# All rows of the array for the spread of the decay sums and for the decay gate's products

## The chip, the cores and the metric

The kernel runs on one core of a Trainium2 chip, in one launch. The metric is the device time in microseconds; lower is better. Before the change the median of three runs is 1002.88 us (1002.50 to 1004.13).

## What is computed

Two transformer blocks in a row on 256 tokens of width 1024, in float32. The change lies in the second block's mixer, which adds two recurrent mixers of one projection `n @ w_in`: a state-space one (SSD, 16 heads in 2 groups) and a gated linear attention (GLA, 4 heads of 128 keys).

```python
proj = n @ w_in                                   # x, z, q, k, v, r, a1 (16 columns), dt (16 columns), ...
# SSD: dt = softplus(dt_raw + dt_bias); a = -dt * exp(A_log); a_cs = cumsum of a over the chunk
#   L[l, s] = exp(a_cs[l] - a_cs[s]) for l >= s, per head
#   y = (C B^T * L) @ (x * dt) + C @ state * exp(a_cs)
# GLA:
log_alpha = jax.nn.log_sigmoid((a1 @ w_a2 + b_a).astype(jnp.float32)) / GLA_TAU    # w_a2: 16 x 512
bcum = jnp.cumsum(log_alpha.reshape(Bsz, nc, CHUNK, H, dk), axis=2)
q_t = qc * jnp.exp(bcum);  k_t = kc * jnp.exp(-bcum);  k_h = kc * jnp.exp(b_last - bcum)
```

`L` needs the running sum of each head along the free axis on every partition; the kernel makes that by a product with a matrix of ones, here called the spread. `a1 @ w_a2` are the decay gate's products.

## The kernel before

All matrices come as 314 weight units of 128 x 1024 numbers (`load`, L87): SP transfers a unit, ScalarE casts its high part to fp32r (`wh`, L94), VectorE subtracts (`wl`, L95), and a product is three TensorE passes, high x high, high x low, low x high (L104 is the one line that issues every product, L108 every transpose). Four `raw` and eight `wh` and `wl` buffers let the units run ahead of the products.

The second block (`block2`) makes the z gate, then `dt_gate`, then `ssd`. `dt_gate` projects a1 and dt, transposed, into one PSUM tile of 48 rows in use (a1, a1, dt), copies it to `xT`, turns it by two transposes, computes dt and the decays `a`, and leaves in `csT` the running sums of 16 heads on rows 0 to 15, and their low parts on rows 32 to 47.

`ssd` pulls its large products from a stream (`stream2`), one piece at each `pump`: the convolved blocks c0, c1, the product v0, then `gla_decays`, then c2, c3, v1, q0, k0 and so on. Between the pumps it states the decay work: `prepare` turns c0 and c1 (c2 and c3 for the second group) by transposes, multiplies by dt and D into X and Y, and makes the chunk state; `decays` makes for four heads at a time a factor `bd` on GpSimd (`csT` times a selector), the spread product with `ones48`, a triangle product that adds the mask, four exponentials on ScalarE and a multiplication by C B on VectorE; `products` applies this tile `L` to X. There are eight such tiles.

What stands where on each engine is set by the Tile framework: `schedule_with_timeline_sim=True` has it place the instructions in the order of a simulated timeline, and give each tile one of its tag's buffers when that is free in this timeline. The tag `k2` has 14 buffers; X, Y, the states, `L`, `bd`, the convolutions and their tanh all take theirs from it. On the chip every engine then runs its instructions in that fixed order.

`gla_decays` begins with the gate: four products of 16 rows, `pb[:16, ...]` (the parameters, L1029) with `a1T` (the first 16 rows of `xT`), in float32, into two PSUM tiles of the tag `acc`, each read by ScalarE with its bias; then the logarithms, the running sums on VectorE and the exponentials. The convolution of a block is `conv` (L875 ff.): on each half an activation with the last tap (L883), three VectorE steps (L885), then a tanh (L269) and a closing product (L888).

Of the kernel before, what the change touches and what calls it, by code (L numbers as in the profile page):

```python
# [11 lines left out]
F32 = mybir.dt.float32  # L12
F32R = mybir.dt.float32r
# [3 lines left out]
OP = mybir.AluOpType  # L17
AX = mybir.AxisListType.X

P = 128  # L20
# [6 lines left out]
C_ID, C_TRI, C_RST, C_INV, C_MC, C_AV, C_I94, C_BM, C_SEL, C_N = 0, 128, 256, 512, 584, 614, 616, 646, 654, 670  # L27
# [3 lines left out]
B_CONV, B_BA, B_DTB, B_AL, B_D, B_A2, B_N = 0, 60, 64, 80, 96, 112, 624  # L31
# [18 lines left out]
class Builder:  # L50
# [221 lines left out]
    def start(self):  # L272
        nc, d = self.nc, self.d
        self.xr = [self.T("xr", [P, 1024]) for _ in range(2)]
        for q in range(2):
            nc.sync.dma_start(self.xr[0][:, q * 512:(q + 1) * 512], d["x"][0:P, q * 512:(q + 1) * 512])  # L276
        self.g_mix = self.gain(G_MIX, nc.sync)
        self.cst = self.T("cst", [P, C_N])
        self.ident = self.cst[:, C_ID:C_ID + P]
        nc.sync.dma_start(self.ident, d["cst"][:, C_ID:C_ID + P])  # L280
        self.tri = self.cst[:, C_TRI:C_TRI + P]
        self.rst = self.cst[:, C_RST:C_RST + 256]
        self.cb = self.T("cb", [P, 3, P], BF16)
        self.cm = self.T("cm", [P, 64], mybir.dt.int32)
        self.posi = self.T("posi", [P, 2], I32)
        self.mhalf = self.T("mhalf", [P, 16])
        nc.vector.memset(self.mhalf, -0.5)
        self.ones = self.T("ones", [P, P])
        nc.vector.memset(self.ones, 1.0)
        self.ones48 = self.T("ones48", [48, P], F32R)  # L290
        nc.scalar.copy(self.ones48, self.ones[:48])

    def rope_tables(self):
        nc = self.nc
# [500 lines left out]
    def dt_gate(self, hT, pb):  # L795

        nc = self.nc
        ps = self.PS()
        ws = self.load("w_dta", 0, P, 0, 8)
        for k, (wh, wl) in enumerate(ws):  # L800
# [1 line left out]
            self.mm(ps[:, :256], wh, hi, k == 0, False)  # L802
            self.mm(ps[:, :256], wh, lo, False, False)
            self.mm(ps[:, :256], wl, hi, False, k == 7)
        xT = self.T("ropes", [48, 256])
        nc.scalar.copy(xT, ps[:48, :256])
        x = self.PS()
        for t in range(2):
            self.tr(x[:, t * 48:(t + 1) * 48], xT[:, t * P:(t + 1) * P])
        x = x[:, :96].rearrange("p (t c) -> p t c", t=2)  # L810
        a1T = xT[:16]

        u = self.T("dtu", [P, 2, 16])
        nc.vector.tensor_tensor(u, x[:, :, 32:48], pb[:, None, B_DTB:B_DTB + 16].broadcast_to((P, 2, 16)), op=OP.add)
        e, s, s2, dt = [self.T(f"dt{i}", [P, 2, 16]) for i in range(4)]
        nc.scalar.activation(e, u, AF.Abs)
        nc.scalar.activation(e, e, AF.Exp, scale=-1.0)
# [10 lines left out]

        A = self.T("dtA", [P, 16])
        nc.scalar.activation(A, pb[:, B_AL:B_AL + 16], AF.Exp)  # L830
        a2 = self.T("dta", [P, 2, 48])
        nc.vector.memset(a2, 0.0)
        for t in range(2):
            for j in (0, 32):
# [1 line left out]
        a = a2[:, :, 0:16]  # L836
# [3 lines left out]
        for t in range(2):  # L840
            ps = self.PS()
            self.mm(ps[:, 0:16], self.tri, a[:, t], True, True)
            nc.vector.tensor_scalar(ncs[:, t], ps[:, 0:16], -1.0, None, op0=OP.mult)
            if t == 1:
                nc.scalar.activation(ecs, ps[:, 0:16], AF.Exp)
            else:
                self.mm(ps[:, 16:32], self.ones, a[:, 0], True, True)
                nc.vector.tensor_tensor(eds, ps[:, 16:32], ncs[:, 0], op=OP.add)
                nc.scalar.activation(eds, eds, AF.Exp)

        csT = self.T("ropec", [48, 2, P], F32R)
        ps = self.PS()
        for t in range(2):
            self.mm(ps[:48, t * P:(t + 1) * P], a2[:, t], self.tri, True, True)
        pv = ps[:48, :256].rearrange("p (t n) -> p t n", t=2)
        nc.scalar.copy(csT, pv)
        nc.vector.tensor_sub(csT[32:48], pv[32:48], csT[32:48].bitcast(F32))

# [61 lines left out]
    def ssd(self, hT, pb, dts, z, dec):  # L920
        nc = self.nc
        dt, dh, csT, ncs, ecs, eds, a1T = dts
# [3 lines left out]
        ps = self.PS()  # L926
# [27 lines left out]
        def decays(g, t, q):  # L954
            ts = slice(t * P, (t + 1) * P)
            if q == 0:
                pc = self.PS()
                self.mm(pc[:, :P], BT[:, g, ts], CT[:, g, ts], True, True)
                cbts[g, t] = self.T("cbt", [P, P], bufs=2)
                nc.scalar.activation(cbts[g, t], pc[:, :P], AF.Copy, scale=0.25)  # L960
            h0 = 8 * g + 4 * q
            pl = self.PS()
            L = self.T("k2", [P, 4, P])
            bd = self.T("k2", [48, 4, P], F32R)
            nc.gpsimd.tensor_tensor(bd, csT[:, t:t + 1].bitcast(F32).broadcast_to((48, 4, P)),
                                    self.cst[:48, C_SEL + h0:C_SEL + h0 + 4, None].broadcast_to((48, 4, P)), op=OP.mult)
            self.mm(pl, self.ones48, bd.rearrange("p a b -> p (a b)"), True, False)
            self.mm(pl.rearrange("p (a b) -> p a b", a=4), self.cb[:, 0], self.cb[:, 2:3].broadcast_to((P, 4, P)), False, True)
            for j in range(4):
                nc.scalar.activation(L[:, j], pl[:, j * P:(j + 1) * P], AF.Exp, bias=ncs[:, t, h0 + j:h0 + j + 1])  # L970
            nc.vector.tensor_tensor(L, L, cbts[g, t][:, None, :].broadcast_to((P, 4, P)), op=OP.mult)
            Ls[g, t, q] = L
# [46 lines left out]
    def gla_decays(self, pb, a1T):  # L1019


        nc = self.nc
        ch = lambda x: x.rearrange("p h (c n) -> p (h c) n", n=64)
        us, es, ks = [[self.T("gd", [P, 2, 256]) for _ in range(2)] for _ in range(3)]
        for i, (u, e) in enumerate(zip(us, es)):
            ps = self.PS("acc")
            for f in range(2):
                h = 2 * i + f
                self.mm(ps[:, f * 256:(f + 1) * 256], pb[:16, B_A2 + h * P:B_A2 + (h + 1) * P], a1T, True, True)  # L1029
                nc.scalar.activation(u[:, f], ps[:, f * 256:(f + 1) * 256], AF.Identity, bias=pb[:, B_BA + h:B_BA + h + 1])  # L1030
            nc.scalar.activation(e, u, AF.Abs)
            last = nc.scalar.activation(e, e, AF.Exp, scale=-1.0)
# [224 lines left out]
def layout(inp):  # L1257

    A = {k: np.asarray(v) for k, v in inp.items()}
# [8 lines left out]
    W["w_dta"] = np.concatenate([w2[:, slice(*o2[k])] for k in ("a1", "a1") + ("dt",) * 6], 1)  # L1268
# [12 lines left out]
    a2[:16] = A["gla_w_a2_2"][0]  # L1281
# [68 lines left out]
```

## Time and profile before

| what | value |
| --- | --- |
| median of 3 runs | 1002.88 us |
| the profiled execution's own time | 1002.88 us |
| its span, first to last instruction | 1000.8 us |
| TensorE (PE) busy, 6404 products and transposes | 980.3 us, 98% |
| VectorE (DVE) | 653.8 us, 65% |
| ScalarE (ACT) | 508.4 us, 51% |
| GpSimd (POOL) | 51.1 us, 5% |
| mean granted TensorE clock | 0.997 |
| HBM read | 173.33 MB, 174 GB/s over the span |

Busy time of TensorE is the union of its products' durations, which overlap: a product's price in a dense stretch is the distance from its start to the next one's. The chain of work that ended last goes through TensorE for 95% of the span. In the timelines a row of several instructions has its count at the end, and a name's buffer numbers are left out. In the rows below `hh`, `hl` are the high and low part of the block's input, `acc`, `sm`, `po` PSUM tiles, `gd` and `k` (for `k2`) SBUF tiles, `par` the parameters.

### The profile page before, as it was taken

How to read it: one execution, taken by the hardware profiler on the slowest of the kernel's cores; microseconds unless marked ns; L12 is line 12 of the kernel's file. 1: busy time of each engine (PE TensorE's matmuls, PEld its weight loads, DVE VectorE, ACT ScalarE, POOL GpSimd, SP SyncE). 2: the span in 40 equal slices, each digit the busy share in tenths (PEclk: the TensorE clock that was granted, in tenths of full speed). 3: DMA queues.
4: the chain of work that ended last, by engine and by line, in shares of the span. 5: the costliest groups of instructions: out<-in, count | busy, mean ns of one | idle time of the engine just before them, and what ended most of it. 6: DMA issues, size and time to landing. Idle time of an engine off the chain costs nothing.

```text
span 1000.8 us, 16162 instructions
## 1 busy us (share of the span) xinstructions
PE 980.3 (98%) x6404; PEld 877.1 (88%) x6404; DVE 653.8 (65%) x969; ACT 508.4 (51%) x792; POOL 51.1 (5%) x77
## 2 busy tenths in 40 slices
PE   6999999999999999999999999999999999999997
PEld 5888998887898999789888899998998878999995
DVE  6887667766655555678778776576756466555543
ACT  5766446444654444555774545454545355444432
POOL 0000000000000000100010131100000000000000
PEclk9999999999999999999999999999999999999998
DMA  8757643243756566375445453753665156656531
GB/s 290 262 167 272 205 152 118 85 147 111 233 182 191 193 220 197 111 247 190 146 150 169 150 167 105 258 186 124 220 196 177 59 186 221 206 170 201 180 126 42
DMA packets 49547, 175.43 MB, mean 175 GB/s; under 512 B 5952, under 2 KB 6336, under 8 KB 49472
## 3 DMA queue, kind: packets, MB, share of 16 engines
q1 hardware_dynamic: 47088, 167.01, 50.5%
q0 software_dynamic: 2096, 6.87, 2.2%
q8 instruction: 50, 0.82, 0.3%
q10 hardware_dynamic: 288, 0.52, 0.1%
q14 instruction: 25, 0.20, 0.1%
HBM read 173.33 MB, written 1.05 MB: 174 GB/s over the span
## 4 chain that ended last, share of the span: by engine, by line
PE 95%; DVE 1%; issue 1%; ACT 1%; DMA 1%; SPq 0%; POOLq 0%; POOL 0%; ACTq 0%
PE acc L104 68%; PE sm L104 23%; PE sm L108 3%; PE po L104 2%; DMA raw<-in_wbig_dram 1%; ACT wh L94 1%; DVE wl L95 0%; ACT hh L111 0%; DVE gd L503 0%; DVE k L328 0%; DVE hl L111 0%; DVE k L346 0%; DVE k L111 0%; SPq L198 0%; SPq L276 0%
## 5 line engine op out<-in xcount | busy, mean ns | idle before, releaser
L95 DVE TENSOR_TENSOR wl<-raw,wh 128x1024 fp32r<-128x1024 f32 (+1 forms) x314 | 382.1, 1228 | 222.7 <-ACT wh L94 221.4
L94 ACT CAST wh<-raw 128x1024 fp32r<-128x1024 f32 (+1 forms) x314 | 325.8, 1049 | 306.0 <-PE acc L104 135.8
L104 PE MATMUL acc<-hh,wh 128*128 128x256 f32 x736 | 207.0, 283 | 0.4 <-ACT hh L111 0.4
L104 PE MATMUL acc<-hh,wl 128*128 128x256 f32 x736 | 207.2, 282 | 0.0
L104 PE MATMUL acc<-hl,wh 128*128 128x256 f32 x736 | 206.9, 282 | 0.0
L104 PE MATMUL acc<-wl,hh 128*128 128x512 f32 (+1 forms) x400 | 157.2, 395 | 1.2 <-DVE wl L95 1.2
L104 PE MATMUL acc<-wh,hh 128*128 128x512 f32 (+1 forms) x400 | 156.5, 397 | 1.9 <-ACT hh L111 1.9
L104 PE MATMUL acc<-wh,hl 128*128 128x512 f32 (+1 forms) x400 | 155.8, 396 | 0.0
L104 PEld LDWEIGHTS acc<-hh,wh 128*128 128x128 f32 x736 | 137.7, 188 | 1.9 <-ACT hh L111 0.5
L104 PEld LDWEIGHTS acc<-hl,wh 128*128 128x128 f32 x736 | 138.3, 188 | 0.7 <-issue 0.5
L104 PEld LDWEIGHTS acc<-hh,wl 128*128 128x128 f32 x736 | 138.1, 188 | 0.4 <-issue 0.3
L104 PE MATMUL sm<-hh,wl 128*128 128x256 f32 x488 | 136.4, 280 | 0.0
L104 PE MATMUL sm<-hl,wh 128*128 128x256 f32 x488 | 136.4, 279 | 0.0
L104 PE MATMUL sm<-hh,wh 128*128 128x256 f32 x488 | 136.2, 279 | 0.0
L104 PEld LDWEIGHTS acc<-wh,hh 128*128 128x128 f32 x400 | 75.6, 189 | 19.3 <-ACT hh L111 3.2
L104 PEld LDWEIGHTS sm<-hl,wh 128*128 128x128 f32 x488 | 91.6, 188 | 0.8
L104 PEld LDWEIGHTS sm<-hh,wh 128*128 128x128 f32 x488 | 91.5, 187 | 0.9
L104 PEld LDWEIGHTS acc<-wl,hh 128*128 128x128 f32 x400 | 75.7, 189 | 18.3 <-DVE wl L95 2.0
L104 PEld LDWEIGHTS acc<-wh,hl 128*128 128x128 f32 x400 | 75.7, 189 | 18.2 <-DVE hl L111 1.2
L104 PEld LDWEIGHTS sm<-hh,wl 128*128 128x128 f32 x488 | 91.5, 187 | 0.0
L104 PE MATMUL acc<-wh,gd 128*128 128x512 f32 x216 | 85.3, 396 | 1.7 <-ACT gd L699 1.3
L104 PE MATMUL acc<-wl,gd 128*128 128x512 f32 x216 | 84.8, 393 | 0.0
(273 smaller groups left out, 1052.6 us busy)
## 6 DMA issues: line engine op xcount, KB each, us to landing
raw<-in_wbig_dram SPq DMA_DIRECT2D x311, 512.0 KB, 4.1
k<-in_gains_dram POOLq DMA_DIRECT2D x18, 256.0 KB, 3.9
k<-in_mem_dram POOLq DMA_DIRECT2D x4, 256.0 KB, 5.6
raw<-in_wbig_dram SPq DMA_DIRECT2D x2, 420.0 KB, 3.8
k<-in_decay_dram POOLq DMA_DIRECT2D x4, 192.0 KB, 4.2
xr<-in_x_dram SPq DMA_DIRECT2D x2, 256.0 KB, 2.9
k<-in_gains_dram SPq DMA_DIRECT2D x2, 256.0 KB, 5.3
xr<-in_x_dram SPq DMA_DIRECT2D x1, 512.0 KB, 7.5
```

Of the source, the lines that this page charges most:

```text
L94: nc.scalar.copy(wh[:, :m], raw[:, :m])
L95: nc.vector.tensor_sub(wl[:, :m], raw[:, :m], wh[:, :m].bitcast(F32))
L104: self.nc.tensor.matmul(out, lhsT, rhs, start=start, stop=stop)
L108: self.nc.tensor.transpose(out, src, self.ident[:n, :n])
```

## The change

It does five things in the second block.

- The spread uses all 128 rows: `csT`, `bd` and the matrix of ones have 128 rows instead of 48; the rows added are zero (`a2`, from which `csT` comes, is cleared and now a k2 tile of 128 columns per half instead of a tile of its own with 48).
- The projection `w_dta` puts its columns in another order (a1, dt, a1, dt, a1, dt, dt, dt), and `xT` and its transposes cover all 128 rows.
- `a1T` is an fp32r tile with the high part of a1 on rows 0 to 15 and 64 to 79 and its low part on rows 32 to 47.
- The gate's weights stand three times on 128 rows; a cast makes them fp32r in a k2 tile, and a subtraction puts their low part on rows 64 to 79. So one fp32r product gives high x high, low x high and high x low at once, in place of a float32 product on 16 rows.
- The float32 matrix of ones is read as the same bits as the fp32r one, through one tile.

```diff
-        self.ones = self.T("ones", [P, P])
-        nc.vector.memset(self.ones, 1.0)
-        self.ones48 = self.T("ones48", [48, P], F32R)
-        nc.scalar.copy(self.ones48, self.ones[:48])
+        ones = self.T("k2", [P, P])
+        nc.vector.memset(ones, 1.0)
+        self.ones = self.T("ones", [P, P], F32R)
+        nc.scalar.copy(self.ones, ones)
...  # dt_gate
-        xT = self.T("ropes", [48, 256])
-        nc.scalar.copy(xT, ps[:48, :256])
+        xT = self.T("k2", [P, 256])
+        nc.scalar.copy(xT, ps[:, :256])
+        a1T = self.T("ropes", [P, 256], F32R)
+        nc.scalar.copy(a1T, ps[:, :256])
+        nc.vector.tensor_sub(a1T[32:64], ps[32:64, :256], a1T[32:64].bitcast(F32))
...
-            self.tr(x[:, t * 48:(t + 1) * 48], xT[:, t * P:(t + 1) * P])
+            self.tr(x[:, t * P:(t + 1) * P], xT[:, t * P:(t + 1) * P])
...
-        a2 = self.T("dta", [P, 2, 48])
+        a2 = self.T("k2", [P, 2, P])
...
-        csT = self.T("ropec", [48, 2, P], F32R)
+        csT = self.T("ropec", [P, 2, P], F32R)
...
-            self.mm(ps[:48, t * P:(t + 1) * P], a2[:, t], self.tri, True, True)
+            self.mm(ps[:, t * P:(t + 1) * P], a2[:, t], self.tri, True, True)
...  # decays
-            bd = self.T("k2", [48, 4, P], F32R)
+            bd = self.T("k2", [P, 4, P], F32R)
...
-            self.mm(pl, self.ones48, bd.rearrange("p a b -> p (a b)"), True, False)
+            self.mm(pl, self.ones, bd.rearrange("p a b -> p (a b)"), True, False)
...  # gla_decays
+        w2 = pb[:, B_A2:B_A2 + 512]
+        a2 = self.T("k2", [P, 512], F32R)
+        nc.scalar.copy(a2, w2)
+        nc.vector.tensor_sub(a2[64:96], w2[64:96], a2[64:96].bitcast(F32))
...
-                self.mm(ps[:, f * 256:(f + 1) * 256], pb[:16, B_A2 + h * P:B_A2 + (h + 1) * P], a1T, True, True)
+                self.mm(ps[:, f * 256:(f + 1) * 256], a2[:, h * P:(h + 1) * P], a1T, True, True)
```

TensorE's order moves with it in `ssd`. The first place is TensorE at the end of v0 (`acc_4942`, `acc_4945` are v0's second half) in the kernel before; `acc_5056` and `acc_5063` are the gate's products, `k_967` is c0, `acc_5090` is c2:

```order
L104 MATMUL acc_4942<-wh_5014,hl_4142 128x512
L104 MATMUL acc_5056<-ropes_4532,par_4325 128x256
L108 MATMUL sm_4902<-cst_69,k_967_4817 128x128 x2
L108 MATMUL sm_4911<-cst_69,k_967_4817 128x128 x2
L104 MATMUL acc_5063<-ropes_4532,par_4325 128x256
L104 MATMUL acc_5090<-hh_4139,wh_5092 128x256
L104 MATMUL acc_5090<-hl_4141,wh_5092 128x256
L104 MATMUL acc_5090<-hh_4139,wl_5093 128x256
```

In the changed program the same place reads so (`k_968` is c0, `k_977` c1, `k_985` the state's factor, `ones_78` the spread):

```order
L104 MATMUL acc_4945<-wh_5017,hl_4142 128x512
L108 MATMUL sm_4905<-cst_69,k_968_4820 128x128 x2
L108 MATMUL sm_4914<-cst_69,k_968_4820 128x128 x2
L108 MATMUL sm_4905<-cst_69,k_977_4893 128x128 x2
L108 MATMUL sm_4914<-cst_69,k_977_4893 128x128 x2
L104 MATMUL sm_4925<-k_985_4923,k_953_4746 128x512
L104 MATMUL sm_4929<-k_951_4734,k_942_4661 128x128
L104 MATMUL sm_4933<-k_992_4935,ones_78 128x512
```

The gate's products are gone from there, c1's transposes, the state and the first spread product have come up, and c2 does not follow.

The second place is TensorE further on in the changed program, where the gate's products now stand (`acc_5062`, `acc_5069`; `acc_5096` is c2); `po_5011` and `po_5237` are the products of the first three decay tiles, `k_991`, `k_1002`, `k_1016`:

```order
L104 MATMUL po_5011<-k_980_4910,k_991_4934 128x64 x4
L104 MATMUL sm_5042<-k_1017_5044,ones_78 128x512
L104 LDWEIGHTS cb_71
L104 MATMUL sm_5042<-cb_71 128x512
L104 MATMUL po_5011<-k_980_4910,k_1002_4983 128x64 x4
L104 MATMUL po_5237<-k_983_4919,k_1016_5043 128x64 x4
L104 MATMUL acc_5062<-ropes_4534,k_1024_5059 128x256
L104 MATMUL acc_5069<-ropes_4534,k_1024_5059 128x256
L104 MATMUL acc_5096<-hh_4139,wh_5098 128x256
```

Between v0's last row and c2's first there are now 21 rows of decay and gate work and none of a large product.

The third place is what the gate's products wait for in the changed program. On ScalarE the cast of the gate's weights (`k_1024<-par`) stands behind the exponentials of three decay tiles:

```order
L973 ACTIVATE k_991_4934<-sm_4933,dtncs_4577 128x128 x3
L973 ACTIVATE k_1002_4983<-sm_4982,dtncs_4577 128x128 [waits DVE_49,PE_49]
L973 ACTIVATE k_1002_4983<-sm_4982,dtncs_4577 128x128 x3
L963 ACTIVATE cbt_5040<-sm_5038 128x128 [waits PE_49]
L973 ACTIVATE k_1016_5043<-sm_5042,dtncs_4577 128x128 [waits PE_49,Pool_49]
L973 ACTIVATE k_1016_5043<-sm_5042,dtncs_4577 128x128 x3
L1031 CAST k_1024_5059<-par_4325 128x512 [waits DVE_49]
L999 ACTIVATE g_909_4489,sc_5139<-k_981_4912 128x512 [waits DVE_49]
L1038 ACTIVATE gd_5053<-acc_5062,par_4325 128x256 [waits PE_49] x2
```

On VectorE the subtraction of the low part stands behind the third tile's product with C B and the first sum into Y:

```order
L974 TENSOR_TENSOR k_991_4934<-k_991_4934,cbt_4931 128x512 [waits Activation_49]
L974 TENSOR_TENSOR k_1002_4983<-k_1002_4983,cbt_4931 128x512 [waits PE_49,Activation_49]
L974 TENSOR_TENSOR k_1016_5043<-k_1016_5043,cbt_5040 128x512 [waits PE_49,Activation_49]
L989 TENSOR_TENSOR k_981_4912<-po_5011,k_981_4912 128x512 [waits PE_49]
L1032 TENSOR_TENSOR k_1024_5059<-par_4325,k_1024_5059 32x512 [waits Activation_49]
```

Before, the gate read the parameters directly and had neither row.

## Rows read from the trace of the kernel before

**Rows 1.** The page, part 1: busy time, share of the span and number of instructions of each engine.

```profile
PE 980.3 (98%) x6404; PEld 877.1 (88%) x6404; DVE 653.8 (65%) x969; ACT 508.4 (51%) x792; POOL 51.1 (5%) x77
```

**Rows 2.** The waits of TensorE over the whole span: who waited for whom, total us, how often, longest us. The longest in total; it is the start of the kernel.

```profile
PE sm L108 <- DVE g L228: 7.9, 1, 7.9
```

**Rows 3.** TensorE's timeline at the end of the product v0: start us, duration us, what. The rows that end in `<-ropes,par` are the decay gate's products, two passes each; `sm<-cst,k` are transposes of the block c0.

```profile
480.09 0.39 PE L104 MATMUL acc<-wh,hl 128*128 128x512 f32 x1
480.41 0.69 PE L104 MATMUL acc<-ropes,par 16*128 16x256 f32 x2
481.04 0.66 PE L108 MATMUL sm<-cst,k 128*128 128x128 f32 x4
481.62 0.69 PE L104 MATMUL acc<-ropes,par 16*128 16x256 f32 x2
...
482.47 0.28 PE L104 MATMUL acc<-hl,wh 128*128 128x256 f32 x1
```

**Rows 4.** TensorE's timeline at the gate's third product.

```profile
485.30 0.28 PE L104 MATMUL acc<-hl,wh 128*128 128x256 f32 x1
485.51 0.69 PE L104 MATMUL acc<-ropes,par 16*128 16x256 f32 x2
...
486.35 0.28 PE L104 MATMUL acc<-hh,wh 128*128 128x256 f32 x1
```

**Rows 5.** TensorE's timeline at one spread product (`<-k,ones`), which the triangle product (`sm<-cb`) follows.

```profile
526.47 0.28 PE L104 MATMUL acc<-hh,wh 128*128 128x256 f32 x1
526.59 0.28 PE L104 MATMUL acc<-hl,wh 128*128 128x256 f32 x1
526.79 0.49 PE L104 MATMUL sm<-k,ones 48*128 48x512 f32 x1
527.22 0.39 PE L104 MATMUL sm<-cb 128*128 128x512 bf16 x1
527.44 0.60 PE L108 MATMUL sm<-cst,k 128*128 128x128 f32 x4
```

**Rows 6.** Groups of TensorE's instructions by line and shape, whole span: count | busy us, mean ns of one.

```profile
L104 PE MATMUL sm<-k,ones 48*128 48x512 f32 x8 | 4.0, 496 | 0.0
L104 PE MATMUL sm<-hh,gd 128*128 128x512 f32 x8 | 3.5, 433 | 0.0
```

**Rows 7.** ScalarE's timeline, single rows: cast of a weight unit's high part, the tanh of the block c1, the copy of the state product out of PSUM, and the four exponentials of one decay tile.

```profile
481.00 1.05 ACT L94 CAST wh<-raw 128x1024 fp32r<-128x1024 f32 x1
...
485.41 0.63 ACT L269 ACTIVATE k<-k 128x512 f32<-128x512 f32 x1 [2.53 <-issue]
...
502.25 0.57 ACT L952 COPY k<-sm 128x512 f32<-128x512 f32 x1
...
507.19 1.15 ACT L970 ACTIVATE k<-sm,dtncs 128x128 f32<-128x128 f32 x4 [0.23 <-PE sm L104]
```

**Rows 8.** VectorE's timeline, single rows: low part of a weight unit twice, the last three steps of the convolution of c1, its closing product, two of the products with dt and D, and the product of a decay tile with C B.

```profile
479.32 1.22 DVE L95 TENSOR_TENSOR wl<-raw,wh 128x1024 fp32r<-128x1024 f32 x1
...
482.08 1.82 DVE L95 TENSOR_TENSOR wl<-raw,wh 128x1024 fp32r<-128x1024 f32 x1 [0.64 <-ACT wh L94]
483.82 1.51 DVE L885 SCALAR_TENSOR_TENSOR k<-acc,par,k 128x255 f32<-128x255 f32 x3
486.07 0.69 DVE L888 SCALAR_TENSOR_TENSOR k<-k,k 128x512 f32<-128x512 f32 x1 [0.74 <-ACT k L269]
...
490.29 0.69 DVE L944 TENSOR_TENSOR k<-sm,dt 128x512 f32<-128x512 f32 x1 [0.35 <-PE sm L108]
490.90 0.68 DVE L946 TENSOR_TENSOR k<-sm,dth 128x512 f32<-128x512 f32 x1
...
508.96 0.68 DVE L971 TENSOR_TENSOR k<-k,cbt 128x512 f32<-128x512 f32 x1
```

**Rows 9.** TensorE's timeline, three pieces of the decay work with the start of what follows each: transposes of c1, the state product with the C B product, the products of one decay tile.

```profile
489.87 0.60 PE L108 MATMUL sm<-cst,k 128*128 128x128 f32 x4
490.23 0.36 PE L104 MATMUL acc<-hl,wh 128*128 128x256 f32 x1
...
499.81 1.24 PE L104 MATMUL sm<-k,k 128*128 128x512 f32 x4
500.80 0.48 PE L104 MATMUL acc<-wh,hh 128*128 128x512 f32 x1
...
511.73 1.00 PE L104 MATMUL po<-k,k 128*128 128x64 f32 x8
512.54 0.36 PE L104 MATMUL acc<-hh,wh 128*128 128x256 f32 x1
```

**Rows 10.** TensorE's timeline at the kernel's first dense products.

```profile
10.60 0.80 PE L104 MATMUL acc<-wh,hh 128*128 128x512 f32 x1 [0.79 <-ACT hh L111]
...
15.12 0.63 PE L104 MATMUL acc<-wh,hh 128*128 128x512 f32 x1
15.55 0.58 PE L104 MATMUL acc<-wl,hh 128*128 128x512 f32 x1
15.97 0.40 PE L104 MATMUL acc<-wh,hl 128*128 128x512 f32 x1
```

**Rows 11.** Busy us (count) of PE, PEld, DVE, ACT and POOL, granted TensorE clock, DMA share and GB/s in two stretches after the last product (the last one starts at 993.17).

```profile
995.00:996.00 1.00, 0.00 (x0) 0.00 (x0) 0.26 (x2) 0.09 (x2) 0.55 (x1) 0.78 0.00 0
996.00:997.00 1.00, 0.00 (x0) 0.00 (x0) 0.71 (x1) 0.68 (x1) 0.00 (x0) 0.50 0.00 0
```

More of the change, by code (lines that the diff above doesn't have):

```diff
@@ L804, in dt_gate @@
             self.mm(ps[:, :256], wl, hi, False, k == 7)
-        xT = self.T("ropes", [48, 256])
-        nc.scalar.copy(xT, ps[:48, :256])
+        xT = self.T("k2", [P, 256])
[3 more added lines that the diff above has]
+        nc.vector.tensor_sub(a1T[32:64], ps[32:64, :256], a1T[32:64].bitcast(F32))
         x = self.PS()
         for t in range(2):
-            self.tr(x[:, t * 48:(t + 1) * 48], xT[:, t * P:(t + 1) * P])
-        x = x[:, :96].rearrange("p (t c) -> p t c", t=2)
-        a1T = xT[:16]
+            self.tr(x[:, t * P:(t + 1) * P], xT[:, t * P:(t + 1) * P])
+        x = x[:, :256].rearrange("p (t c) -> p t c", t=2)
         u = self.T("dtu", [P, 2, 16])
-        nc.vector.tensor_tensor(u, x[:, :, 32:48], pb[:, None, B_DTB:B_DTB + 16].broadcast_to((P, 2, 16)), op=OP.add)
+        nc.vector.tensor_tensor(u, x[:, :, 16:32], pb[:, None, B_DTB:B_DTB + 16].broadcast_to((P, 2, 16)), op=OP.add)
         e, s, s2, dt = [self.T(f"dt{i}", [P, 2, 16]) for i in range(4)]
@@ L846, in dt_gate @@
             else:
-                self.mm(ps[:, 16:32], self.ones, a[:, 0], True, True)
+                self.mm(ps[:, 16:32], self.ones.bitcast(F32), a[:, 0], True, True)
                 nc.vector.tensor_tensor(eds, ps[:, 16:32], ncs[:, 0], op=OP.add)
                 nc.scalar.activation(eds, eds, AF.Exp)
-        csT = self.T("ropec", [48, 2, P], F32R)
+        csT = self.T("ropec", [P, 2, P], F32R)
         ps = self.PS()
         for t in range(2):
-            self.mm(ps[:48, t * P:(t + 1) * P], a2[:, t], self.tri, True, True)
-        pv = ps[:48, :256].rearrange("p (t n) -> p t n", t=2)
+            self.mm(ps[:, t * P:(t + 1) * P], a2[:, t], self.tri, True, True)
+        pv = ps[:, :256].rearrange("p (t n) -> p t n", t=2)
         nc.scalar.copy(csT, pv)
@@ L963, in decays @@
             L = self.T("k2", [P, 4, P])
-            bd = self.T("k2", [48, 4, P], F32R)
-            nc.gpsimd.tensor_tensor(bd, csT[:, t:t + 1].bitcast(F32).broadcast_to((48, 4, P)),
-                                    self.cst[:48, C_SEL + h0:C_SEL + h0 + 4, None].broadcast_to((48, 4, P)), op=OP.mult)
-            self.mm(pl, self.ones48, bd.rearrange("p a b -> p (a b)"), True, False)
+            bd = self.T("k2", [P, 4, P], F32R)
+            nc.gpsimd.tensor_tensor(bd, csT[:, t:t + 1].bitcast(F32).broadcast_to((P, 4, P)),
+                                    self.cst[:, C_SEL + h0:C_SEL + h0 + 4, None].broadcast_to((P, 4, P)), op=OP.mult)
+            self.mm(pl, self.ones, bd.rearrange("p a b -> p (a b)"), True, False)
             self.mm(pl.rearrange("p (a b) -> p a b", a=4), self.cb[:, 0], self.cb[:, 2:3].broadcast_to((P, 4, P)), False, True)
@@ L1267, in layout @@
     W["w_in2"] = np.concatenate([w2[:, slice(*o2[k])] for k in ("x", "z", "q", "k", "v", "r", "gs", "gg")], 1)
-    W["w_dta"] = np.concatenate([w2[:, slice(*o2[k])] for k in ("a1", "a1") + ("dt",) * 6], 1)
+    W["w_dta"] = np.concatenate([w2[:, slice(*o2[k])] for k in ("a1", "dt", "a1", "dt", "a1", "dt", "dt", "dt")], 1)
     for n, m in (("ck1", "cmp_k_w1"), ("cv1", "cmp_v_w1"), ("pa", "w_proj_a"), ("pb", "w_proj_b"), ("w_out", "w_out"), ("w_up", "w_up"),
@@ L1280, in layout @@
     a2 = np.zeros((P, 512), np.float32)
-    a2[:16] = A["gla_w_a2_2"][0]
+    for r in range(3):
+        a2[32 * r:32 * r + 16] = A["gla_w_a2_2"][0]
     D["parb"] = np.concatenate([
```

## The prediction

> **What bounds the kernel now.** I read the page's busy times first, then TensorE's waits, then its timeline between the second block's convolutions and its decays, and last the order of the changed program. TensorE is busy for 98% of the span [rows 1], and the longest of its waits is the 7.9 us at the very start [rows 2]. So a product made cheaper is worth its full time, and any hole torn into TensorE's order costs its full length, since no later slack gives it back. The reader should look for two things in the timelines: how far apart products start (their durations overlap, so the distance from start to start is the price), and what TensorE would have to do if the next row of its order were not ready.
>
> **What the change saves on TensorE.** A spread product reads 48 rows now. Around one of them the starts stand 0.20, 0.43 and 0.22 us apart [rows 5]. A 128x256 product of that stream takes 0.12 (526.47 to 526.59) and the triangle product, as wide as the spread one, 0.22. So 0.08 goes before and 0.21 behind the 48-row product; over the whole piece it is 0.85 - 0.12 - 0.22 - 0.23 = 0.28, which I take. Its duration points the same way: 496 ns against 433 of a full-row product of that width [rows 6]. Eight of them give 2.2 us. The bounds are 0 (rows are not the cause) and 0.29 each.
>
> The Trainium skill has rules for both ends. "TensorEngine Tiling (Array Packing)", Key Properties, says that changing the tiling mode drains TensorE; by that the change recovers the gaps. "TensorE: Matmul & The Clock Gate", Part 2, says of weight loads that the row count doesn't matter; by that the 0.28 stays, and the sum below comes out 1.9 us higher. The trace has the gaps, but no row shows a full-row spread product, so this second rule is a rival.
>
> A gate product is two passes on 16 rows in 4-byte mode. From 485.30 to 486.35 stand one 128x256 product, one gate product and a second 128x256 product [rows 4]: 1.05 us. With one fp32r pass of 128x256 it would be 3 x 0.117 = 0.35. That is 0.70 saved, four times 2.8 us. In the dt gate two transposes and a four-pass product lose their 48-row form: I take 0.2 (bounds 0 and 0.4, four edges at 0.1). If nothing else moved, the sum would be 2.2 + 2.8 + 0.2 = 5.2 us less.
>
> **What the change moves.** It does more than that. The gate's weights are now first copied to a tile of the k2 pool. That cast reads only parameters which are long there, so the wait that it carries on ScalarE is for the buffer: it is the one of the first decay tile (k_991), free only after VectorE and TensorE have used it. Everything that the program states later, c2's products too, was ordered behind it. So between v0's last product and c2's first, TensorE's order now holds only decay work, each piece waiting for another engine. Before, the gate's products and c0's transposes stood there and c2 followed at once [rows 3]. I walk that stretch in the clock of the trace of before:
>
> - 480.32: v0's last product starts at 480.09 [rows 3] and lasts 0.23. c0's transposes follow, to 480.9. Then TensorE waits for c1.
> - c1: the cast of the last weight unit ends at 482.05 [rows 7]. VectorE has its low part ahead of c1's second half; 1.22 [rows 8], to 483.3. (It was 1.82 before.) Three steps 1.51, the tanh 0.63, the closing product 0.69 [rows 7, 8]: 486.15.
> - c1's transposes at 486.2. VectorE reads them 0.42 after their start (489.87 to 490.29) [rows 8, 9]: 486.6. Four products at 0.61 (490.29 to 490.90) and one of 0.69 for the chunk state: 489.75.
> - State and C B products 0.99 [rows 9]; their copies on ScalarE, 0.57 for the larger [rows 7], I allow 0.75 for both: 491.5. The first spread product lies beside this.
> - Exponentials 1.15, product with C B 0.68: 493.3. The first decay tile's products 0.81 [rows 9]: 494.1. The third spread product stands behind them, with its triangle 0.65: 494.75. Its exponentials 1.15 (the second tile's lie before them): 495.9.
> - VectorE then does three things in a row of 0.68 each: the third tile's product with C B, the sum into Y, and the low part of the gate's weights (32 rows; 512 columns as the others). 497.95. The cast itself, about 0.57, is beside the first of them.
> - Two gate products 0.25, and c2 starts at 498.2.
>
> That is 17.9 us after 480.32. In it TensorE does work that it did elsewhere before, at these old prices: c0's transposes and two gate products, 480.32 to 482.47 less 0.12, 2.03; c1's transposes 0.36 + 0.08; state and C B 0.99 + 0.1; a second C B 0.2; three spread products with triangle 0.73 each, 2.2; three tiles' products 0.81 + 0.1 each, 2.7 [rows 3, 5, 9]. Sum 8.7. So the hole is 17.9 - 8.7 = 9.2 us, with the savings of three spread and two gate products already inside. Outside remain five spread products, 1.4, two gate products, 1.4, and the dt gate's 0.2: 3.0. Net at an unchanged clock: 9.2 - 3.0 = 6.2 us more.
>
> **The clock.** TensorE is idle for some 5 us while c1 is finished. At the end of the kernel its granted clock is 0.78 in 995 to 996 and 0.50, that is 1.2 GHz, from 996 on; its last product had begun at 993.17 [rows 11]. At the kernel's start the dense 128x512 products, from 10.60 on, still start 0.43 apart at 15.12, and 0.23 apart only from about 15.97 [rows 10]. So I expect 1.2 GHz from within the idle time to some time after c2's start. Its price in the chain: the TensorE pieces there, 0.36 + 0.99 + 0.65 + 0.81 + 0.25, about 3.1, double at most; some lie beside copies, and I take half, 1.5. After c2's start, 4 to 5 us at half pace lose 2. Bounds for both together: 0 and 3.1 + 2.5.
>
> Sum: 6.2 + 1.5 + 2.0 = 9.7 us. The profiled run took 1002.88 (its span is 1000.8), and so did the median of the runs. Forecast 1002.88 + 9.7 = 1012.6, say **1012.5**.
>
> **Costs at nothing.** The extra ScalarE copy and VectorE subtraction in the dt gate (256 columns each, below 0.69) and the wider memset lie beside c0's and BT's products; the dt products stand eight 128x256 products later in TensorE's order, 0.9 us. Without that cover they would cost up to 1.4. GpSimd's factor of the spread product has 128 rows and as many columns; the third one has until 494.1. After the hole c2, c3 and v1 have their weight units ready, so no transfer is late; next in line is c2's convolution on VectorE, which now runs beside the decay gate's logarithms and sums and must be closed when v1 is through, 96 products at 0.117 and 48 at 0.23, 22 us after c2's start.
>
> **The rivals.**
> - *It does what it says, faster.* No hole: 5.2 us less, 997.7. This needs c1 closed on VectorE by 480.3, when v0 ends. In the trace it closes at 486.07 + 0.69 [rows 8], and the weight cast before it waits for v0 itself. From a lead of 5 us on the sign turns. Against it: that wait. Chance 0.03.
> - *Hole and savings cancel to within 0.2%.* The hole would have to be some 5 us, about c1's wait alone, with the decay pieces running beside each other. Against it: the order of the rows. 1002.9 to 1004.5; 0.03.
> - *The clock stays up or returns at once* (the transposes and state product count enough): 1002.88 + 6.2 = 1009.1. For it: TensorE is not quite idle from 486 on. 0.22.
> - *Rows are not the cause.* The gaps round the spread products stay, 1.4 outside the hole and 0.5 for the two on its chain: 1014.4. It is the second of the skill's rules above. The gate still saves its second pass. 0.14.
> - *A second hole.* c2's or c3's transposes come before their convolution is closed, because VectorE and ScalarE have the gate's logarithms, and weights in between. Walking the new order with these prices I find 1 to 2 us of slack; 3 us late gives 1015.5. 0.13.
>
> **How the numbers follow.** The forecast has 0.45. Range 1007 to 1017: the low end is the unchanged clock with 2 us off my chain (the pieces beside each other), the high end the second hole with 1.5 us more clock loss. It leaves out the two rivals of the other signs and tails of the rest, about 0.15. About 0.2%, 2 us, is what a measurement here can tell from no change. Faster 0.03, same 0.03, slower 0.94.
>
> **What would show it.** Right: in the new timeline TensorE has an idle stretch of some 5 us just after v0, released by VectorE's closing product of c1, then short ones released by ScalarE's exponentials and VectorE; c2 starts 18 to 20 us after v0; TensorE's granted clock falls in that stretch; spread products are followed after 0.23, not 0.43. Wrong: c2's products follow v0 within 10 us, or TensorE's waits sum to less than 8 us more than before, or the time is at or below 1004.9.

## The result and the profile after

The changed kernel takes **1013.38 us** (median of 4 runs, 1012.25 to 1013.91), the kernel before 1002.86 beside it: a ratio of 1.0099, 95% interval [1.0086, 1.0112] (the medians alone divide to 1.0105). The forecast was 1012.5. The profiled execution took 1013.91, its span is 1012.0. Medians below are of all runs of a version; the ratios leave out one run each of experiments 5, 8 and 10 and one of the kernel before, which took 1202 to 3902 us.

TensorE is still busy for 97% of the span. Its longest waits, to set beside [rows 2]:

```profile
...
PE sm L108 <- DVE k L891: 5.3, 1, 5.3
PE sm L104 <- DVE k L951: 2.8, 1, 2.8
...
PE po L104 <- DVE k L989: 1.9, 1, 1.9
PE acc L104 <- ACT gd L699: 1.9, 1, 1.9
```

Three of these are new and on VectorE: its closing product of c1 (L891), its factor of the chunk state (L951), its sum into Y (L989). The forecast had put an idle stretch behind v0, released by the first. TensorE's timeline from v0's last product to c2's first, beside [rows 3, 5, 9]:

```profile
479.94 0.39 PE L104 MATMUL acc<-wh,hl 128*128 128x512 f32 x1
480.17 0.60 PE L108 MATMUL sm<-cst,k 128*128 128x128 f32 x4
486.08 1.11 PE L108 MATMUL sm<-cst,k 128*128 128x128 f32 x4 [5.31 <-DVE k L891]
490.03 2.47 PE L104 MATMUL sm<-k,k 128*128 128x512 f32 x4 [2.84 <-DVE k L951]
...
496.26 0.47 PE L104 MATMUL sm<-k,ones 128*128 128x512 f32 x1
...
499.67 1.08 PE L104 MATMUL po<-k,k 128*128 128x64 f32 x8 [1.87 <-DVE k L989]
500.56 0.48 PE L104 MATMUL acc<-ropes,k 128*128 128x256 f32 x2
500.88 0.28 PE L104 MATMUL acc<-hh,wh 128*128 128x256 f32 x1
```

Read the bracket at a row's end: it names what the product waited for. The chain is there in the order in which the prediction walked it, and c2's first product (the last row) starts 20.9 us after v0's last (the first row), 20.7 after c0's transposes. Before, it started 2.2 us after v0's last, which [rows 3] has at 480.09:

```profile
482.25 0.39 PE L104 MATMUL acc<-hh,wh 128*128 128x256 f32 x1
```

Near the end of the chain stand three VectorE steps in a row, beside [rows 8], and on ScalarE the cast of the gate's weights (L1031):

```profile
498.07 0.63 ACT L1031 CAST k<-par 128x512 fp32r<-128x512 f32 x1
...
498.23 0.69 DVE L974 TENSOR_TENSOR k<-k,cbt 128x512 f32<-128x512 f32 x1 [1.91 <-ACT k L973]
498.84 0.68 DVE L989 TENSOR_TENSOR k<-po,k 128x512 f32<-128x512 f32 x1
499.56 0.68 DVE L1032 TENSOR_TENSOR k<-par,k 32x512 fp32r<-32x512 f32 x1
```

TensorE's last wait ends with the second of the three (L989). The third decay tile's products (499.67) and then the gate's (500.56) follow, and the low part of the weights (L1032) is done by then, at 500.24. The cast starts as soon as the exponentials ahead of it are through, with no idle time before it. So it is the place that the cast was given in the order that costs the time here, and not a wait for its buffer on the chip.

The granted clock in that stretch (busy us of PE, PEld, DVE, ACT, POOL, then PEclk, DMA share, GB/s):

```profile
484.00:488.00 4.00, 1.11 (x4) 0.71 (x4) 2.44 (x5) 0.63 (x1) 0.72 (x1) 0.59 0.39 131
488.00:492.00 4.00, 1.97 (x3) 0.96 (x4) 1.89 (x4) 0.00 (x0) 0.32 (x1) 0.50 0.00 0
492.00:496.00 4.00, 3.35 (x15) 2.15 (x13) 1.06 (x2) 3.10 (x11) 1.04 (x1) 0.63 0.00 0
496.00:500.00 4.00, 2.13 (x18) 1.84 (x17) 2.05 (x4) 1.65 (x5) 0.00 (x0) 1.00 0.00 0
```

It falls to 0.50 (1.2 GHz) in the idle time and is back at 1.00 before c2 starts. The savings are there too. In the kernel before, this row follows the gate product that starts at 485.51 in [rows 4]:

```profile
486.13 0.38 PE L104 MATMUL acc<-hh,wl 128*128 128x256 f32 x1
```

In the changed kernel, a gate product, and a spread product in the dense stream, whose gaps before were 0.20 and 0.43 [rows 5]:

```profile
503.35 0.28 PE L104 MATMUL acc<-ropes,k 128*128 128x256 f32 x1
503.46 0.28 PE L104 MATMUL acc<-hh,wh 128*128 128x256 f32 x1
...
551.87 0.39 PE L104 MATMUL acc<-wh,hl 128*128 128x512 f32 x1
552.10 0.39 PE L104 MATMUL sm<-k,ones 128*128 128x512 f32 x1
552.33 0.39 PE L104 MATMUL sm<-cb 128*128 128x512 bf16 x1
```

The gate product is followed after 0.11, before after 0.62. The spread product is followed after 0.23 and starts 0.23 after a product as wide: no gap is left.

**Where the time went.** Both programs run 5584 products on weight units. The start of the n-th of them in one trace against the other, from one mark to the next, gives this account in us (worked out from the two traces, with the times of the kernel before; the marks are the 240th, 2220th, 2460th, 3360th, 4500th, 4560th and the last):

| stretch | after against before |
|---|---|
| up to 70 us: kernel start | +0.9 |
| 70 to 441 us | 0.0 |
| to 474 us: dt gate, c0, c1, head of v0 | -1.1 |
| to 636 us: v0's end, decays, the rest of both state parts | +9.3 |
| to 833 us | 0.0 |
| to 846 us | +2.1 |
| to the end | 0.0 |

The sum is 11.2, as the spans have it. The start is a wait for an input transfer, 8.6 instead of 7.9 us; experiment 6, which has the whole change, shows -0.4 there, so it is not the change. The +2.1 lies at a wait that stood there before: TensorE waits 1.9 instead of 1.3 us for ScalarE (L699), whose cast ahead of it waited 1.8 us for a weight transfer, and this time the clock falls behind it:

```profile
846.00:850.00 4.00, 4.00 (x12) 3.13 (x11) 2.65 (x6) 1.21 (x3) 0.00 (x0) 0.57 0.60 214
```

Of the profiles of the twelve kernels below only experiment 8's has that too (+2.2); it is not part of the change.

### The profile page after: what moved, and what is told of

It is laid out like the page before. It is cut to its first block, busy times and chain, and to the rows that moved or that the text cites. A ratio compares the mean times of both kernels' runs of the same rounds, so it can differ in the third digit from the quotient of the medians.

```text
span 1012.0 us, 16156 instructions
## 1 busy us (share of the span) xinstructions
PE 979.6 (97%) x6400; PEld 878.1 (87%) x6400; DVE 653.1 (65%) x971; ACT 508.8 (50%) x794; POOL 53.7 (5%) x77
## 4 chain that ended last, share of the span: by engine, by line
PE 91%; DVE 3%; DMA 2%; ACT 2%; issue 1%; SPq 0%; POOLq 0%; POOL 0%; ACTq 0%
PE acc L104 65%; PE sm L104 21%; PE sm L108 2%; DMA raw<-in_wbig_dram 2%; PE po L104 2%; DVE wl L95 1%; ACT wh L94 1%; ACT hh L111 0%; ACT k L973 0%; DVE gd L503 0%; DVE k L974 0%; DVE k L328 0%; DVE k L947 0%; DVE k L949 0%; DVE hl L111 0%
## 5 line engine op out<-in xcount | busy, mean ns | idle before, releaser
L94 ACT CAST wh<-raw 128x1024 fp32r<-128x1024 f32 (+1 forms) x314 | 325.5, 1048 | 303.7 <-PE acc L104 125.7
```

The costliest lines, as they stand in the source:

```text
L94: nc.scalar.copy(wh[:, :m], raw[:, :m])
```

## The experiments

The theory on record: the cast into a k2 buffer tears the hole, full rows save 2.2 us and the stacked gate 2.8. Each was taken apart. Times are medians, ratios against runs of the kernel before on the same chip, with their 95% intervals.

**1. The gate's weights in a tile of their own.**

```diff
-        a2 = self.T("k2", [P, 512], F32R)
+        a2 = self.T("gw", [P, 512], F32R)      # and sc=32 becomes sc=30
```

> The changed kernel, with the gate's cast weights in a tile of their own instead of a k2 buffer (two small scratch buffers fewer make the room). Theory (the wait for the k2 buffer alone tears the hole, and rows cost what the timeline says): c2's products follow v0's within 3 us, TensorE's waits on VectorE behind v0 are gone, and all 5.2 us of savings show: 997.7 us (997 to 999). Rival 1, rows of the spread product cost nothing: only gate and dt gate save, 999.9. Rival 2, the hole comes from something else (the wider GpSimd factors, c1's closing): it stays, above 1009.

Measured 1009.72, ratio 1.0058 [1.0043, 1.0072]. The hole is gone: c2 follows v0's last product after 1.1 us. But by the ratios 11 of the expected 15 us did not come, and no rival had it so. The trace has two new losses: a wait of 3.2 us near 592, and 128x256 products that start 0.1187 apart on average instead of 0.1178. Experiments 4, 5, 9, 10 and 11 take these up.

**2. The copy alone.** The kernel before, with a plain copy of the gate's weights in a k2 buffer.

```diff
+        a2 = self.T("k2", [P, 512])
+        nc.scalar.copy(a2, pb[:, B_A2:B_A2 + 512])
...
-                self.mm(ps[:, f * 256:(f + 1) * 256], pb[:16, B_A2 + h * P:B_A2 + (h + 1) * P], a1T, True, True)
+                self.mm(ps[:, f * 256:(f + 1) * 256], a2[:16, h * P:(h + 1) * P], a1T, True, True)
```

> The kernel before with one thing of the change alone: the gate's weights are copied (plainly, no split, no stacking) to a k2 buffer, and the gate's products read 16 rows of that copy. Theory: the same hole at the old prices. The stretch from v0 to c2 is 20.7 us in the changed kernel; without VectorE's 0.68 for the low part, with 3 x 0.28 and 2 x 0.70 more for the old products, about 22, less the 8.7 of work that it displaces: +13, 1016 (1014 to 1018). Rival (the wider products and the split make the hole): no hole, 1002.9, at most 0.6 more for the copy.

Measured 1020.66, ratio 1.0172 [1.0155, 1.0188]. The copy tears the hole without anything else of the change; from c0's transposes to c2's first product are 22.5 us. The excess over 1016 is the clock: here it does not come back before c2 starts.

```profile
504.00:506.00 2.00, 2.00 (x10) 2.00 (x11) 1.08 (x2) 0.22 (x2) 1.52 (x2) 0.50 0.00 0
...
508.00:510.00 2.00, 2.00 (x7) 1.33 (x7) 0.00 (x0) 0.69 (x2) 0.00 (x0) 0.50 0.00 0
510.00:514.00 4.00, 4.00 (x26) 4.00 (x26) 0.01 (x1) 2.34 (x4) 0.00 (x0) 0.70 0.00 0
```

c2 starts at 503.88, and the clock column stays at 0.50 to past 510; the products are back at full pace at 512.4. That is some 8.5 us at half pace, which lose near 4 us. That is the forecast's price after c2's start, absent in the changed kernel and double its size here.

**3. The spread alone on 128 rows.**

```diff
-            bd = self.T("k2", [48, 4, P], F32R)
+            bd = self.T("k2", [P, 4, P], F32R)
...
-            self.mm(pl, self.ones48, bd.rearrange("p a b -> p (a b)"), True, False)
+            self.mm(pl, self.onesr, bd.rearrange("p a b -> p (a b)"), True, False)
```

> The kernel before with the spread alone on 128 rows (sums' transposes, factor and ones too); gate as before. Theory (48 rows cost the gaps around the product): 8 x 0.28 = 2.2 us less, 1000.6, and products behind the spread start after 0.23. Rival (the gaps have another cause): 1002.9.

Measured 1001.38, ratio 0.9977 [0.9966, 0.9989]: 2.3 us less. This is the one version that beats both kernels.

**4. The gate alone.** As in experiment 1, but with 48 rows in the spread (`bd` 48 rows, `self.ones[:48]`).

> The kernel with the own tile for the gate's weights, but its spread product reads 48 rows of the same tiles. Theory: the gate's 4 x 0.70 and the dt gate's 0.2, 3.0 us less than before, 999.9; 2.2 more than with the full-row spread. Rival (rows of the spread are not its cause): the same time as with the full-row spread.

Measured 1011.07, ratio 1.0079 [1.0066, 1.0091]. Against experiment 1 the difference of the ratios is 0.0021, 2.1 us, give or take 1.9: it agrees with experiment 3, but is the weaker evidence for the spread. The absolute time is not the 999.9 expected: the same two new losses stand in this trace.

**5. The gate's weights in a gd buffer.** No tile moves, and it is not a k2 buffer.

```diff
-        a2 = self.T("k2", [P, 512], F32R)
+        a2 = self.T("gd", [P, 2, 256], F32R).rearrange("p a b -> p (a b)")
```

> The changed kernel with the gate's cast weights in one of the free gd buffers: no k2 buffer, and no tile moved (the version with the tile of its own had its weight tiles 64 bytes per partition lower against the activations, and its 128x256 products started 0.1187 apart instead of 0.1178 through the whole kernel). The instructions stand as in that version on ScalarE, VectorE, GpSimd and SyncE. Theory (first hole gone; the loss left is a second hole, TensorE waiting 3.2 us for ScalarE's eviction of an accumulator at about 592 with half clock behind it, and the slower rate came from where the tiles lie): the rate is 0.1178 again, some 3.5 us less than with the own tile, and the wait at 592 stays: 1006 (1004 to 1007.5). Rival (the rate is the run's or the order's, not the place's): 1009 to 1010 with 0.1187 again. Rival (the wait at 592 is a consequence of the rate): 998.

Measured 1005.11, ratio 1.0020 [1.0007, 1.0034], as the theory had it. The products start 0.1178 apart again. What is left is the second hole; TensorE's waits from 480 on, its timeline there, and ScalarE's:

```profile
PE acc L104 <- ACT g L269: 3.4, 1, 3.4
PE sm L104 <- ACT k L1097: 1.0, 1, 1.0
```

```profile
589.32 0.28 PE L104 MATMUL acc<-hh,wl 128*128 128x256 f32 x1
593.02 0.39 PE L104 MATMUL acc<-hh,wh 128*128 128x256 f32 x1 [3.43 <-ACT g L269]
...
594.04 0.41 PE L104 MATMUL acc<-hh,wh 128*128 128x256 f32 x1
594.25 0.42 PE L104 MATMUL acc<-hl,wh 128*128 128x256 f32 x1
```

```profile
590.82 0.63 ACT L999 ACTIVATE g<-k 128x512 f32<-128x512 f32 x1 [1.67 <-DVE k L997]
...
591.45 1.03 ACT L94 CAST wh<-raw 128x1024 fp32r<-128x1024 f32 x1
592.39 0.59 ACT L269 ACTIVATE g<-acc 128x512 f32<-128x512 f32 x1
```

The product needs an accumulator. ScalarE's tanh (L269) frees it, but stands behind the square of the SSD's norm (L999), which waits for VectorE, and behind the cast of a weight unit (L94). Behind the wait some 15 products start 0.21 apart: half clock. 3.4 + 1.0 + 15 x 0.095 = 5.8 us. Up to this wait the savings had come: the 3064th product on weight units, with the same work ahead of it in both programs, starts at 583.58, which is 4.95 us earlier than before, counted from the 2220th. From there to the 3360th the trace loses 6.7, of which 0.9 are not among the three terms.

**6. The hole filled.** 40 products more, of the ones against the activations, into an accumulator that nobody reads.

```diff
         yield from v(0)
+        fill = self.PS("acc")
+        for _ in range(40):
+            self.mm(fill[:, :256], self.ones, hT.parts(0)[0], True, True)
```

> The changed kernel with 40 products more (128x256, the ones against the activations, into an accumulator that nobody reads) between v0 and c1's transposes, where TensorE waits 5.3 us; 40 x 0.118 = 4.7 us fit. No other instruction moves. Theory (the hole's price is the wait plus half clock behind it): the fill is free and the clock stays at 2.4 GHz to c2's start, so the stretch from v0 to c2 is 18 us instead of 20.7, and the time 1010.6 (1010 to 1011.5). Rival (the clock costs nothing there, since the pieces wait for other engines): 1013.4, as the changed kernel. Rival (the fill delays c1's transposes): above 1014.

Measured 1012.35, ratio 1.0095 [1.0082, 1.0108], against 1.0099 of the changed kernel: no difference.

```profile
479.21 0.39 PE L104 MATMUL acc<-wh,hl 128*128 128x512 f32 x1
...
481.47 3.35 PE L104 MATMUL acc<-hh,ones 128*128 128x256 f32 x26
485.35 0.66 PE L108 MATMUL sm<-cst,k 128*128 128x128 f32 x4 [0.54 <-DVE k L891]
489.06 2.47 PE L104 MATMUL sm<-k,k 128*128 128x512 f32 x4 [3.05 <-DVE k L954]
...
500.42 0.42 PE L104 MATMUL acc<-hh,wh 128*128 128x256 f32 x1
```

c1's transposes start 5.91 us after v0's last product is through, exactly as without the fill (480.17 to 486.08): 4.7 us of work went in free (14 products ahead of c0's transposes, the 26 shown behind them). c1's transposes run in 0.66 instead of 1.11. But the next wait is 0.2 longer, the clock falls 4 us later, and the state product takes the same 2.47. c2 starts 21.2 us after v0's last product starts, against 20.9, and its first nine steps run at half clock. In this one profile the stretch from v0's end to the 3360th product costs 10.6, against 9.3 of the changed kernel. So filling this one wait buys nothing; whether the clock matters in the rest of the chain this run does not tell, since it was low there again.

**7. The cast stated early, in a k2 buffer.**

```diff
     def stream2(self, hT, pb, dec, a1T):
+        w2 = pb[:, B_A2:B_A2 + 512]
+        a2 = self.a2 = self.T("k2", [P, 512], F32R)
+        self.nc.scalar.copy(a2, w2)
+        self.nc.vector.tensor_sub(a2[64:96], w2[64:96], a2[64:96].bitcast(F32))
         w = "w_in2"
```

> The changed kernel with the cast and the split of the gate's weights stated at the head of the stream of products, ahead of c0, in a k2 buffer that is free by then. Theory (what tears the hole is which k2 buffer the cast gets, not that it is one): gate products follow v0 at once, no wait at 480; 997.7 if no other wait opens, and 1004 to 1006 if the same wait for ScalarE as with the own tile opens near 592. Rival (any k2 buffer taken from the decays tears a hole, here for the decay tiles): above 1009.

Measured 1005.02, ratio 1.0021 [1.0012, 1.0030]. No wait at 480, the same wait of 3.2 us near 592. So the k2 pool is not the trouble by itself. The same cast, stated where a buffer is free, tears no hole; which buffer it gets, and behind whom it is placed for that, decides.

**8. The cast and the split on GpSimd**, on top of experiment 5 (`nc.gpsimd.tensor_copy`, `nc.gpsimd.tensor_sub`).

> As the version with the gd buffer, with the cast and the split of the gate's weights on GpSimd instead of ScalarE and VectorE. Theory: they are far off any path; what counts is the order of the rest, which changes on ScalarE. If the wait near 592 is one of that order, it goes or shrinks: 997.7 to 1002. Rival (it comes from TensorE running ahead of VectorE's chain by the 3 us that the gate saves, whatever ScalarE's order): the wait stays, within 1 us of the gd version.

Measured 1005.42, ratio 1.0022 [1.0013, 1.0031], with a wait of 3.7 us at the same place, and the tanh still stands behind the norm and the weight cast. So the gate's cast on ScalarE is not the cause; the order of the rest stays open here.

**9. The gate stated behind c1**, on top of experiment 5.

```diff
-        for x in (conv(0), conv(1)):
-            yield from x
-        yield from v(0)
+        yield from conv(0)
+        yield from conv(1)
         dec += self.gla_decays(pb, a1T)
-        for x in (conv(2), conv(3), v(1)):
+        for x in (v(0), conv(2), conv(3), v(1)):
```

> The version with the gd buffer, with the gate stated behind c1 instead of behind v0. In the versions with the gate behind v0, the last decay products stand behind 3012 to 3063 weight products in TensorE's order, in the kernel before behind 2968 to 3027; here they stand behind 2968 to 3027 again. Theory (the wait near 592 is made by that order: 36 to 44 stream products, 4 to 5 us, stand ahead of the last decay pieces, so TensorE meets an accumulator that ScalarE's tanh, queued behind the SSD's norm, has not freed): no such wait, and all savings show: 1003 less 5.2, 997.8 (997 to 999.5). Rival (the wait is the 5 us saved: VectorE's chain bounds that stretch, in any order): still 3 us and more of waits there, 1003 to 1006.

Measured 1002.91, ratio 0.9992 [0.9983, 1.0001]. The wait near 592 is gone, and the time is still not 997.8. TensorE's waits from 455 to 700 now are these, and the clock behind the first:

```profile
PE acc L104 <- ACT gd L1037: 2.0, 2, 1.2
PE sm L104 <- DVE k L950: 1.1, 1, 1.1
```

```profile
472.00:476.00 4.00, 3.97 (x11) 3.17 (x12) 2.55 (x6) 2.36 (x5) 0.00 (x0) 0.61 0.54 176
```

The gate's products now stand one behind the other between c1 and v0, and wait for ScalarE to take their sums out of the accumulators. 3.1 us of waits and some 1.5 at half clock take up most of the 5.2.

That the wait is gone does not by itself prove the order theory: the savings were lost before 480, so TensorE came to that place no earlier than in the kernel before (594.66 against 594.02). The distances decide it. In the kernel before, from the last decay tile's products to the tanh and to the product that needs the accumulator:

```profile
583.12 1.00 PE L104 MATMUL po<-k,k 128*128 128x64 f32 x8
...
594.02 0.28 PE L104 MATMUL acc<-hh,wh 128*128 128x256 f32 x1
```

```profile
590.92 0.58 ACT L269 ACTIVATE g<-acc 128x512 f32<-128x512 f32 x1
```

TensorE has 10.9 us of work in between, and the tanh is through after 8.4. It is 10.9 and 8.8 in experiment 3, which reaches this place 2.4 us earlier and does not wait, and 10.9 and 9.0 here. In experiment 5 those decay products start at 582.77, and the order leaves 36 products fewer between: 6.7 us of work against 10.2 to the tanh's end. So it is the order, on TensorE and on the engines behind the tanh, and not the lead alone.

**10. The early cast, the gate stated behind c0.** As experiment 9, with experiment 7's cast and c1 behind the gate too.

> The version with the early cast in a k2 buffer, with the gate stated behind c0. TensorE's order of the last decay products is again that of the kernel before (2968 to 3027 weight products ahead of them). Theory (order): 997.8 (997 to 999.5), with no wait for ScalarE's tanh near 592. Rival (VectorE's chain bounds): 1003 to 1006. Rival (any k2 buffer for the gate costs the decays a wait): a new wait on VectorE between 480 and 500.

Measured 1007.84, ratio 1.0045 [1.0031, 1.0058]. Again no wait near 592, and no wait between 480 and 500; but a new one of 6.5 us earlier, for VectorE's convolution to free an accumulator:

```profile
PE acc L104 <- DVE k L898: 6.5, 1, 6.5
```

**11. Only the tiles moved.** The changed kernel with `sc=30` instead of `sc=32`; the order of all instructions is the same, the tiles behind `sc` lie 64 bytes per partition lower.

> The changed kernel with 30 instead of 32 small scratch buffers, so that all tiles allocated behind them (weights among them) lie 64 bytes per partition lower, as in the version with the tile of its own; every instruction stands in the same place. Theory (the rate of 0.1187 from start to start of 128x256 products comes from where the weight tiles lie against the activations): about 3.6 us more than the changed kernel, 1016 to 1017. Rival (it came from that version's own run or order): 1013.4 and 0.1178.

Measured 1018.74, ratio 1.0151 [1.0135, 1.0166]: by the ratios 5 us more than the changed kernel for nothing but addresses. In the same stretch of the third stage, the last row is 50 products behind the first, first of the changed kernel, then of this one:

```profile
729.72 0.28 PE L104 MATMUL acc<-hh,wl 128*128 128x256 f32 x1
...
735.61 0.28 PE L104 MATMUL acc<-hl,wh 128*128 128x256 f32 x1
```

```profile
729.80 0.28 PE L104 MATMUL acc<-hh,wh 128*128 128x256 f32 x1
...
735.73 0.28 PE L104 MATMUL acc<-hh,wl 128*128 128x256 f32 x1
```

0.1178 and 0.1186 apiece. In the changed kernel all these steps are 0.117 to 0.119, here they spread from 0.115 to 0.122. TensorE's products are the same in the same order in both.

**12. The spread on 64 rows**, on top of experiment 3 (`bd` and the ones on 64 rows).

> The version with the full-row spread alone, with the spread product and its factor on 64 rows (of which 48 carry the sums, the rest zeros); every instruction stands in the same place. Theory (any product on part of the rows costs the switch, whatever the count): the gaps of the 48-row product come back, 0.20 before and 0.43 behind instead of 0.12 and 0.23, 2.2 us more than with full rows: 1003.4. Rival (48 is the trouble, 64 rows as a half of the array are free): no gaps, 1001.4.

Measured 1003.20, ratio 0.9998 [0.9989, 1.0007]. The gaps are back, 0.20 before and 0.43 behind:

```profile
527.27 0.28 PE L104 MATMUL acc<-hl,wh 128*128 128x256 f32 x1
527.47 0.49 PE L104 MATMUL sm<-k,onesr 64*128 64x512 f32 x1
527.90 0.39 PE L104 MATMUL sm<-cb 128*128 128x512 bf16 x1
```

Of the three counts that ran, 48 and 64 rows cost the same and 128 nothing. So it is not the 48 that costs; why less than the full rows does, no run shows.

## Why the prediction was right, point by point

- **The hole and its cause: shown.** The k2 copy alone makes it (experiment 2), another buffer or an earlier cast removes it (1, 5, 7). That the buffer was the first decay tile's, as the prediction says, no run shows by itself. The walk gave 17.9 us at an unchanged clock; it measures 20.7. Closing c1 was expected 5.83 after the start and came at 5.85 (485.33 + 0.69). The factor of the chunk state was 0.3 late. Then the state and C B products, 0.99 in the walk, took 2.47 at half clock, and the exponentials started 13.25 instead of 11.2 after the start. Behind them come 0.4 more up to the third tile's exponentials, and 0.4 at the end, where the third decay tile's products stand ahead of the gate's; the walk had left them off its chain. The prediction's sign, c2 18 to 20 us after v0, was missed by 0.9; its other signs came out.
- **The clock: right that it falls, wrong in both sizes.** In the chain I took 1.5; the excess over the walk is 2.8, of which 2.1 arise up to the first exponentials, where TensorE's pieces run at half clock. After c2's start I took 2.0; it was 0, since the clock had come back at about 495. So 3.5 for both stands against 2.8 in all: the misses nearly cancel, which is luck. Experiment 2 shows that the second term exists (near 4 us there), experiment 6 that 0.9 of it comes back with a slightly other stretch. No run has the 2.0.
- **The displaced work and the savings: right, the gate's a little too large.** Experiment 3 gives 2.3 for the term of 2.2, and 12 takes it away again. The rival that rows are not the cause is out. The bound of the dt gate was 0.4 at most; it is 0.45 in experiments 5 to 8. In the changed kernel's trace that stretch gained 1.1; the rest is a pace of 0.114 instead of 0.118 in c0 and c1, which experiment 10's trace has there too and the others not, and for which no run shows a cause. The gate's term of 2.8 is 2.3 to 2.4 in experiment 5: of the 4.95 us saved there by 583, 0.44 is the dt gate's and 2.2 the spread's. No version's time is lower by it.
- **The sum.** From v0's end to the last chunk the change costs 9.3; walk, displaced work and outside savings without the dt gate gave 20.7 - 8.7 - 2.8 = 9.2 with the measured chain, which bears out the displaced work and these savings together, not each by itself. With the 1.1 gained ahead of it the change costs 8.2 in this trace, 1.5 less than the 9.7 forecast. The other 3.0 of its 11.2, at the start and near 846, are not the change's; that the time came within 1 us of the forecast is in part luck.
- **The step that failed** is one that the result did not test: "if nothing moved, 5.2 us less". I had taken the hole as the only thing between the savings and the time. With the hole away the time is 1005, with the second one away too 1003, and there other waits had come. The rival *It does what it says* asked only for c1 to be closed by 480.3; in the orders that came out without the hole, TensorE met ScalarE's tanh 110 us later, or other waits earlier. The changed kernel has no second hole; where one opened, the rival of that name had looked at c2's and c3's transposes, and it lay at an accumulator.

What stays open: which order of the rest would let the gate's saving through to the end, and what the clock alone costs inside the chain.

## What to carry to other kernels

A tile taken from a rotating pool may have to wait for the last reader of its buffer; where a scheduler orders the program, what is stated later may line up behind it, so look first at whose buffer a new tile gets. On an engine that is busy for 98% of the time a saving can still be lost: the spread's 2.3 us came through by itself, the gate's did not. After each saving ask which accumulator, tanh or convolution is met that much earlier. And change one thing at a time, addresses included: here moving tiles by 64 bytes cost about as much as the change was to save.

## What the runs showed that I had not expected

- Where tiles lie moves the pace of plain products: 64 bytes per partition lower, 0.1178 became 0.1186 to 0.1187, some 5 us of the whole (experiments 1, 4 and 11, the others not). What in the addresses does it, no run tells.
- A product on 64 rows costs the same gaps as one on 48: 0.28 us each among full-row products (527.27 to 528.12 in experiment 12, less the products' own 0.12, 0.23 and 0.22).
- GpSimd's factor barely notices its rows: 1.17 us on average with 48 and with 64 rows (the kernel before, experiment 12) and 1.20 with 128 (experiment 3). It is 1.30 in the changed kernel, where the rest of the program differs too.
- A wait of some 3 us on TensorE can cost more than its length: in experiment 5 the clock fell within a microsecond after the products had resumed, and stayed at half for 3 us of dense work, 1.4 us more.
